# Attention with four query buffers instead of two, and queries asked for three groups in advance

## The chip, the cores and the metric

The kernel runs on one core of a Trainium2 chip. The metric is the time on the device of one execution, in microseconds (us). Engines are named as in the profile: PE (matrix products), DVE (vector), ACT (activations), POOL (GpSimd), SP (the queue that issues most of the transfers). PEld is the loading of PE's weights.

## What is computed

One layer of a decoder in float32, for 2048 tokens of width 1024: attention with latent projections beside a short convolution, an output projection, a layer of 32 experts of which each token takes two, a gated embedding, and norms. The change lies in the attention alone. For each of 8 heads and each block of queries:

```python
s = (einsum('bqhd,bkhd->bhqk', q_nope[:, q0:q1], k_nope[:, :q1])
     + einsum('bqhr,bkr->bhqk', q_rope[:, q0:q1], k_rope[:, :q1]))
...
s = jnp.where(mask, s * scale, -jnp.inf)
pr = jax.nn.softmax(s, axis=-1)
outs.append(einsum('bhqk,bkhd->bqhd', pr, v[:, :q1]))
```

The mask is causal, so that a query sees the keys up to its own place.

## The kernel before

The layer runs in stages: `project` makes queries, keys and values and stores them in DRAM, each split into two float32r parts, high and low; `attention` reads them back; then come the output projection, the routing, the experts and the last norm. Stages follow one another on the engines, but the transfers and the tail of one run beside the head of the next, and a buffer of one stage lies where a buffer of the stage before it lay, and must wait for that one's last use.

**Groups and steps.** Attention goes head by head (h = 0 to 7), and in a head by groups g = 0 to 3 of 512 queries, written (h,g) here. Group (h,g) needs the key chunks 0 to g of 512 keys each, so that it has 4(g + 1) steps: 4, 8, 12, 16 for the four groups, 40 a head. In each step PE makes the scores of 128 queries against 512 keys (L629 to L631: three products, high by high, high by low, low by high), transposes a block of probabilities of 15 steps ago (L655), and multiplies a block of 22 steps ago with the values (L666). DVE takes maxima (L634) and the low part of the transposed blocks (L66), ACT the exponentials (L643) and the high part (L65). The order of every engine but SP's landings is fixed by the text of the program; it is written out by hand (`manual_schedule`).

**Loads.** SP issues in order, and an issue waits until the buffer that it fills is free; what stands behind it waits too. `load_q(h, g)` (L596, L597) fetches 384 KB of queries into one of 2 buffers (`qp`, L569). `load_k(h, c)` (L585, L586) fetches 384 KB of keys into one of 6. `load_v(h)` (L590) fetches 1 MB into one of 2. They are asked for in `scores`, at a group's first step (L601 to L612): at g = 0 the key chunks 2 and 3 of this head; at g = 3 the chunks 0 and 1 and the values of the next head; and last, at each group, the queries of the next one. So the queries of (h,1) are asked for when (h,0), the shortest group, begins, behind two key chunks, and into the buffer that (h-1,3) has just left.

**The end of a group.** When the 16 exponentials of a group are summed, DVE makes the reciprocals (`sm`, L674, L675; 2 buffers). POOL then, in its own order: stores `sm` into DRAM, transposed, in elements of 4 bytes (`rd<-sm`, L681); reads it back along the other axis for 64 partitions (`rb<-rd`, L683), for which it waits until the store has landed; takes the values' sum from `lo`, where ACT has copied it out of its bank (L694; 2 buffers): copy (L695), addition (L696), multiplication with `rb` (L697), store of the result (`od<-o`, L698). PE has one bank for the values' sum, so that the next group's first product (L666) waits for ACT's copy, and ACT's copy waits until POOL has done with `lo` of two groups before. On POOL the order of a head is: `rd` and `rb` of (h-1,3); `rd` and `rb` of (h,0); the products of (h-1,3) and of (h,0); `rd`, `rb`, products of (h,1); the same of (h,2). For h = 1 to 4 POOL also issues a clearing store of 2 MB (L711).

Of the kernel before, what the change touches and what calls it, by code (L numbers as in the profile page):

```python
# [31 lines left out]
# rows of the experts' outputs: the first 128 of each expert, then the next 64 of each;  # L32
# those past 192 go in blocks of 128 of their own
# [3 lines left out]
# units of weights on chip, as loaded and split  # L37
# [4 lines left out]
# tiles of p @ w_ple_proj that wait until the experts are done  # L42
# [3 lines left out]
def row_bc(ap, n):  # L46
    """A DRAM row of n elements, read by every partition."""
    return bass.AP(tensor=ap.tensor, offset=ap.offset, ap=[[0, 128], [1, n]])


class Kernel:
# [7 lines left out]
    def split(self, hi, lo, src, lo_eng=None, hi_eng=None, later=None):  # L59
        """hi + lo = src, each of them exact in float32r; lo only noted where it is for later."""  # L60
        nc = self.nc
        if hi_eng:
            hi_eng.tensor_copy(hi, src)
        else:
            nc.scalar.activation(hi, src, AF.Copy)  # L65
        f = lambda: (lo_eng or nc.vector).tensor_tensor(lo, src, hi.bitcast(F32), op=OP.subtract)  # L66
        f() if later is None else later.append(f)

    def mm3(self, ps, terms, start=True, stop=True):
        """ps += sum of (ah + al)^T (bh + bl), al^T bl aside."""  # L70
        mm, n = self.nc.tensor.matmul, len(terms)
        for i, (ah, al, bh, bl) in enumerate(terms):
            mm(ps, ah, bh, start=(start and i == 0), stop=False)  # L73
            mm(ps, ah, bl, start=False, stop=False)  # L74
            mm(ps, al, bh, start=False, stop=(stop and i == n - 1))  # L75

    def acc(self, ps, prods):
        """ps = the sum of products."""
        for i, (l, r) in enumerate(prods):
            self.nc.tensor.matmul(ps, l, r, start=i == 0, stop=i == len(prods) - 1)  # L80

    def rsqrt_steps(self, pool, r, v):
        """r = v ** -0.5, from an integer guess and three Newton steps; stops between two of them."""
        V = self.nc.vector
        t = pool.tile([128, r.shape[1]], F32, name="rsq_t", bufs=2)
        ri = r.bitcast(I32)
        V.tensor_scalar(ri, v.bitcast(I32), 1, None, op0=OP.logical_shift_right)
        yield
        V.tensor_scalar(ri, ri, -1.0, float(0x5F3759DF), op0=OP.mult, op1=OP.add)
        for _ in range(3):  # L90
            yield
            V.scalar_tensor_tensor(t, r, -0.5, r, op0=OP.mult, op1=OP.mult)
            yield
            V.tensor_tensor(t, t, v, op=OP.mult)
            yield
            V.scalar_tensor_tensor(r, t, 1.5, r, op0=OP.add, op1=OP.mult)
# [6 lines left out]
    def rms_steps(self, pool, r, ss, n):  # L103
        """r = 1 / sqrt(ss / n + EPS), by columns."""
        v = pool.tile([128, ss.shape[1]], F32, name="rms_v", bufs=2)
        self.nc.vector.tensor_scalar(v, ss, 1.0 / n, EPS, op0=OP.mult, op1=OP.add)
        yield
        yield from self.rsqrt_steps(pool, r, v)
# [62 lines left out]
    def project(self, st):  # L171
# [52 lines left out]
        # gains and taps as columns: q 0-2, kv 3-4, taps 5-16 (tap, channel tile)  # L224
# [5 lines left out]
        # rows of the rotary tables: frequency, phase in turns, phase; 64 of cosines, 64 of sines  # L230
# [8 lines left out]
        # sums of every 32nd row  # L239
# [26 lines left out]
        def up_weights():  # L266
            # tiles of 128 columns: 0-3 two heads each without rotation, 4-5 the rotated halves of four heads each
# [176 lines left out]
        def start():  # L444
            """The first tokens' way to the first columns, in the order in which they come."""
# [90 lines left out]
    def rope_angles(self, f512, pi, rcol):  # L536
        """Angles within a turn, for positions pi, a row's kind given by rcol."""
# [17 lines left out]
        # a turn more or less where the first guess was a little off  # L555
# [10 lines left out]
    def attention(self, st):  # L566
        tc, nc = self.tc, self.nc
        kp = self.pool(st, "a_k", 6)
        qp = self.pool(st, "a_q", 2)  # L569
# [29 lines left out]
        def scores(h, g, qi, c):  # L599
            """Scores of 128 queries and 512 keys; with the last of a row's, its softmax."""  # L600
            if c == 0 and qi == 0:  # L601
                if (h, g) == (0, 1):
                    load_v(0)
                if g == 0:
                    load_k(h, 2)
                    load_k(h, 3)
                if g == 3 and h + 1 < H:
                    load_k(h + 1, 0)
                    load_k(h + 1, 1)
                    load_v(h + 1)  # L610
                if (h, g) != hg[-1]:
                    load_q(*hg[hg.index((h, g)) + 1])  # L612
                G = groups[h, g] = dict(pt={}, q=qs_.pop((h, g)))
                G["P"] = [(p3 if g == 3 else p012).tile([128, (g + 1) * 512], F32, name=f"P{g}") for _ in range(4)]
                if g == 1 and R1 + h * 512 - 512 in range(R1, R2):
                    clear(R1 + h * 512 - 512)
                G["rs"] = wk.tile([128, 4, NG], F32, name="rs", bufs=3)
# [53 lines left out]
        def sums(h, g):  # L671
            """1 / the softmax's sums."""
            sm = groups[h, g]["sm"] = wk.tile([128, 4], F32, name="sm")
            nc.vector.tensor_reduce(sm, groups[h, g]["rs"][:, :, :g + 1], axis=AX.X, op=OP.add)  # L674
            nc.vector.reciprocal(sm, sm)  # L675

        def sums_row(h, g):
            """The same along the free axis, on a head's partitions."""
# [6 lines left out]
        def normalise(h, g):  # L685
            """o^T of a head and 512 queries."""
# [28 lines left out]
        load_k(0, 0)  # L715
        load_k(0, 1)
        for n in range(len(s_seq) + lag_v):
# [5 lines left out]
            # a group's last product goes first: what comes next waits for its bank  # L723
# [12 lines left out]
    def ring(self, st):  # L736
        """Weights in units of [128, 1024]: NRAW as they come, NSPLIT split, both used in turn."""
# [13 lines left out]
    def split_unit(self, scale=None, pool=False, later=None):  # L751
        """The next unit's parts, its rows multiplied by scale."""
# [16 lines left out]
    def mix_out(self, st):  # L769
# [50 lines left out]
        # constants of the norm and of the routing; router weights, both levels side by side, hi and lo  # L820
# [31 lines left out]
        # kept: weights, expert and rank of a token's two choices  # L852
# [15 lines left out]
        def trans(t):  # L868
            """xn^T, split, two tiles of tokens side by side."""
# [12 lines left out]
        def logits(t):  # L882
            """Router logits of tiles t and t + 1, transposed; the parts of hi and lo weights below each other."""
# [14 lines left out]
        def route(t0, n):  # L898
            """The choices of n tiles of tokens, and their rows; a step at a time."""
# [13 lines left out]
            def first(hot, d, w, k):  # L913
                """The first of the zeros in d, one-hot."""
# [25 lines left out]
            # one-hot experts, ranks among an expert's tokens  # L940
# [27 lines left out]
            # places in the lists; a far token's is past their end  # L968
# [28 lines left out]
        def go(k=-1, ranks=False):  # L997
            """k steps of the routing, or all (-1); past the ranks' products only if told so."""
# [81 lines left out]
        # the last tiles' way to the lists, beside tiles of p @ w_ple_proj  # L1080
# [38 lines left out]
        # counts of tokens, and of blocks of 128 past FAR  # L1119
# [11 lines left out]
        # rows and weights of a token's two choices, nought if it is far  # L1131
# [22 lines left out]
    def ple_prep(self, wk, t, pst, keep=None):  # L1154
        """p^T of a tile, split; or only kept."""
# [27 lines left out]
    def unit_loads(self, most=NRAW):  # L1183
        """Loads of weights as far ahead as there is room."""
# [34 lines left out]
    def gather(self, e, r):  # L1219
        """The rows of an expert's first 128 tokens (r = 0) or the next 64; where there is none, a row is left."""  # L1220
# [17 lines left out]
    def experts(self, st):  # L1238
# [8 lines left out]
        def half(ps, n, out=None):  # L1247
            """The sum of the two halves' rows."""
# [6 lines left out]
        def block(e, more):  # L1255
            """An expert's first 128 rows; with more, 64 others, their hi and lo side by side."""
# [10 lines left out]
            def free(pool=False):  # L1267
                """A unit is done with: the next in line takes its place."""
                self.next_unit(pool)

            def prods(j, r):
                """Unit j's products, for the first rows (r = 0) or the others."""
# [19 lines left out]
            def hidden(f, r):  # L1292
                """The hidden layer's columns of half f, and where they go transposed."""
# [67 lines left out]
            # the places of the expert before's last two units, and of all but the last two of this one's  # L1361
# [28 lines left out]
    def far_experts(self, st):  # L1390
# [3 lines left out]
        # apart from where the experts start  # L1394
# [6 lines left out]
        with tc.If(nov > 0):  # L1401
            cum = wk.tile([128, E], F32, name="cum")
            V.tensor_tensor_scan(cum, self.ones[:, :E], nb, 0.0, op0=OP.mult, op1=OP.add)
            # the expert of a block
# [10 lines left out]
            # rows of the far tokens  # L1415
# [82 lines left out]
    def finish(self, st):  # L1498
# [124 lines left out]
        # sums of squares: of tile t - 2 (after the embedding) and t + 2 (before)  # L1623
# [37 lines left out]
        # the last tile in parts  # L1661
# [86 lines left out]
```

## Time and profile before

| what | us |
|---|---|
| time of three runs: 2479.6, 2501.54, 2488.54; median | 2488.54 |
| span of the profiled execution | 2492.2 |
| PE busy in it | 2313.6 (93%) |
| DVE busy | 1728.2 (69%) |
| ACT busy | 1341.4 (54%) |
| POOL busy | 701.6 (28%) |

The profiled execution is one of its own; its time outside the span is not given, and its span lies 3.7 us above the median of the three runs. Busy time doesn't count waits: an engine that issues a transfer and then waits for another one to land is idle in this table. Attention takes the stretch from 550 to 1085 us. In rows with a bracket, its number is the engine's idle time just before the instruction and the name what ended it.

### The profile page before, as it was taken

The numbers are of one execution on the slowest core, as the hardware profiler recorded it, in microseconds if no ns is written. First come the engines' busy times: TensorE is split into PE (matmuls) and PEld (weight loads), VectorE is DVE, ScalarE is ACT, GpSimd is POOL, SyncE is SP. The second block draws the span as 40 slices with busy tenths as digits, with TensorE's granted clock in tenths as the row PEclk, the third lists the DMA queues.
The fourth block names the chain that finished last, engine by engine and source line by source line (L and its number), as shares of the span: only waits on it lengthen the run. The fifth ranks groups of instructions, "written<-read, shape, count | busy, mean of one in ns | idle before, by whom it ended". The sixth has DMA issues, their size and how long they took to land. (4 is left out here: it accounts for less than half of the span.)

```text
span 2492.2 us, 34982 instructions
## 1 busy us (share of the span) xinstructions
PE 2313.6 (93%) x12058; PEld 1904.2 (76%) x12058; DVE 1728.2 (69%) x3007; ACT 1341.4 (54%) x2409; POOL 701.6 (28%) x671
## 2 busy tenths in 40 slices
PE   7999999989999999979997998999999999999997
PEld 5878787877787777768785777877787878787775
DVE  6746556537777777767676777667666776776887
ACT  5333333326777777742224666656656665665434
POOL 2121212122233333352333233213322232223342
PEclk9999999998999999999998998999999999999999
DMA  7363635355545444465656789778877887784562
GB/s 216 104 207 102 200 98 180 89 164 105 113 109 118 117 80 80 104 136 183 204 176 209 265 284 317 250 236 285 273 225 245 294 277 262 254 298 148 169 203 94
DMA packets 298378, 465.68 MB, mean 187 GB/s; under 512 B 28105, under 2 KB 198130, under 8 KB 298130
## 3 DMA queue, kind: packets, MB, share of 16 engines
q1 hardware_dynamic: 254304, 333.56, 44.6%
q0 software_dynamic: 36304, 105.39, 13.0%
q10 hardware_dynamic: 7522, 23.61, 2.5%
q8 instruction: 133, 2.18, 0.4%
q14 instruction: 115, 0.94, 0.1%
HBM read 369.04 MB, written 97.62 MB: 187 GB/s over the span
## 5 line engine op out<-in xcount | busy, mean ns | idle before, releaser
L66 DVE TENSOR_TENSOR ul<-raw,uh 128x1024 fp32r<-128x1024 f32 x326 | 465.7, 1446 | 189.3 <-ACT uh L65 175.5
L65 ACT ACTIVATE uh<-raw 128x1024 fp32r<-128x1024 f32 x396 | 403.3, 1052 | 85.7 <-PE bank L1286 36.8
L73 PE MATMUL bank<-uh,xh 128*128 128x256 f32 (+1 forms) x768 | 253.4, 330 | 21.1 <-ACT uh L65 12.1
L74 PE MATMUL bank<-ul,xh 128*128 128x256 f32 (+1 forms) x768 | 249.4, 325 | 3.6 <-issue 3.6
L75 PE MATMUL bank<-uh,xl 128*128 128x256 f32 (+1 forms) x768 | 248.8, 324 | 2.6 <-issue 2.6
L66 POOL TENSOR_TENSOR ul<-raw,uh 128x1024 fp32r<-128x1024 f32 x70 | 170.2, 2433 | 278.2 <-ACT uh L65 242.8
L66 DVE TENSOR_TENSOR pt<-tr,pt 128x512 fp32r<-128x512 f32 (+2 forms) x320 | 194.6, 610 | 76.5 <-ACT pt L65 73.3
L65 ACT ACTIVATE pt<-tr 128x512 fp32r<-128x512 f32 (+2 forms) x317 | 168.9, 533 | 116.5 <-PE tr L655 111.9
L634 DVE TENSOR_REDUCE mx<-s 128x1 f32<-128x512 f32 (+2 forms) x320 | 192.7, 603 | 45.5 <-PE s L631 40.1
L73 PE MATMUL mm<-xh,wh 128*128 128x512 f32 x536 | 212.2, 398 | 6.9 <-ACT xh L65 6.9
L75 PE MATMUL mm<-xh,wl 128*128 128x512 f32 x536 | 212.0, 396 | 0.0
L74 PE MATMUL mm<-xl,wh 128*128 128x512 f32 x536 | 211.8, 395 | 0.0
L666 PE MATMUL av<-pt,v 128*128 128x512 f32 (+3 forms) x640 | 207.1, 408 | 1.4 <-ACT lo L694 1.4
L643 ACT ACTIVATE P<-s,mx 128x512 f32<-128x512 f32 (+2 forms) x320 | 198.8, 622 | 11.5 <-DVE mx L639 11.5
L65 ACT ACTIVATE wh<-raw 128x1024 fp32r<-128x1024 f32 x68 | 72.0, 1060 | 219.0 <-PE mm L74 184.7
L655 PE MATMUL tr<-ident,P 128*128 128x128 f32 x1088 | 180.6, 283 | 0.0
L73 PEld LDWEIGHTS bank<-uh,xh 128*128 128x128 f32 x768 | 147.0, 191 | 38.9 <-issue 24.3
L629 PE MATMUL s<-k,q 96*128 96x512 f32 (+2 forms) x320 | 131.9, 412 | 36.2 <-DMA q<-qrd 27.3
L75 PEld LDWEIGHTS bank<-uh,xl 128*128 128x128 f32 x768 | 147.2, 192 | 18.4 <-issue 6.2
L74 PEld LDWEIGHTS bank<-ul,xh 128*128 128x128 f32 x768 | 147.4, 192 | 14.0 <-issue 1.1
L66 DVE TENSOR_TENSOR xl<-tr,xh 128x512 fp32r<-128x512 f32 x160 | 106.0, 684 | 70.8 <-ACT xh L65 69.6
L655 PEld LDWEIGHTS tr<-ident,P 128*128 128x128 f32 x1088 | 134.7, 146 | 24.9 <-issue 2.0
(371 smaller groups left out, 5587.5 us busy)
## 6 DMA issues: line engine op xcount, KB each, us to landing
raw<-in_w_gate_dram SPq DMA_DIRECT2D x128, 512.0 KB
raw<-in_w_up_dram SPq DMA_DIRECT2D x128, 512.0 KB
raw<-in_w_down_dram SPq DMA_DIRECT2D x128, 512.0 KB
raw<-in_w_in_dram SPq DMA_DIRECT2D x68, 512.0 KB
yd<-y POOLq DMA_DIRECT2D x32, 512.0 KB
xr<-in_x_dram SPq DMA_DIRECT2D x16, 512.0 KB
kd<-stg POOLq DMA_DIRECT2D x16, 512.0 KB
vd<-stg POOLq DMA_DIRECT2D x16, 512.0 KB
```

Of the source, the lines that this page charges most:

```text
L65: nc.scalar.activation(hi, src, AF.Copy)
L66: f = lambda: (lo_eng or nc.vector).tensor_tensor(lo, src, hi.bitcast(F32), op=OP.subtract)
L73: mm(ps, ah, bh, start=(start and i == 0), stop=False)
L74: mm(ps, ah, bl, start=False, stop=False)
L75: mm(ps, al, bh, start=False, stop=(stop and i == n - 1))
L629: mm(s, qh, k[:, 0, :w], start=True, stop=False)
L634: nc.vector.tensor_reduce(mx[:, c:c + 1], s, axis=AX.X, op=OP.max, negate=(g == 0))
L643: nc.scalar.activation(G["P"][qi][:, j * 512:j * 512 + s.shape[1]], s, AF.Exp, bias=nm, accum_out=G["rs"][:, qi, j:j + 1])
L655: nc.tensor.transpose(ps[:, jj], G["P"][qi][:, j * 128:j * 128 + 128], self.ident)
L666: mm(G["av"][:, q0:], heads[h]["v"][:, j], G["pt"][jq][:, hl, jj, q0:], start=(j == 0 and hl == 0), stop=(j == 4 * g + 3 and hl == 1))
```

## The change

`qp` has 4 buffers instead of 2. At a group's first step the queries of the group three further on are asked for, before the keys and the values; the line that asked for the next group's queries last is gone. Before the first step the queries of (0,1) and (0,2) are asked for, between and behind the first key chunks. Nothing is computed otherwise. (The rest of the diff takes out comments.)

```diff
-        qp = self.pool(st, "a_q", 2)
+        qp = self.pool(st, "a_q", 4)
...
             if c == 0 and qi == 0:
+                ahead = hg.index((h, g)) + 3
+                if ahead < len(hg):
+                    load_q(*hg[ahead])
                 if (h, g) == (0, 1):
                     load_v(0)
...
-                if (h, g) != hg[-1]:
-                    load_q(*hg[hg.index((h, g)) + 1])
...
         load_q(0, 0)
         load_k(0, 0)
+        load_q(0, 1)
         load_k(0, 1)
+        load_q(0, 2)
```

SP's order where head 1 begins, before: the rows from the values of head 1 (asked for at group (0,3)) to the queries of (1,2). The numbers tell the buffers' uses apart.

```order
L590 DMA v_4575<-vd_83 128x16x128
L596 DMA q_4577<-qd0_72 64x1024
L597 DMA q_4577<-qrd0_76 32x1024
L585 DMA k_4859<-kd0_78 64x1024
L586 DMA k_4859<-krd_82 32x1024
L585 DMA k_4862<-kd0_78 64x1024
L586 DMA k_4862<-krd_82 32x1024
L596 DMA q_4865<-qd0_72 64x1024
L597 DMA q_4865<-qrd0_76 32x1024
```

Here q_4577 holds the queries of (1,0), the two k the chunks 2 and 3 of head 1, and q_4865 the queries of (1,1), last in the line that (1,0) starts. The same place now:

```order
L596 DMA q_4575<-qd0_72 64x1024
L597 DMA q_4575<-qrd0_76 32x1024
L585 DMA k_4578<-kd0_78 64x1024
L586 DMA k_4578<-krd_82 32x1024
L585 DMA k_4581<-kd0_78 64x1024
L586 DMA k_4581<-krd_82 32x1024
L590 DMA v_4584<-vd_83 128x16x128
L596 DMA q_4865<-qd0_72 64x1024
L597 DMA q_4865<-qrd0_76 32x1024
L585 DMA k_4868<-kd0_78 64x1024
L586 DMA k_4868<-krd_82 32x1024
```

Now q_4575, asked for at (0,3), holds the queries of (1,2), and the keys and values of head 1 stand behind it; q_4865, asked for at (1,0), holds those of (1,3), and chunks 2 and 3 of head 1 stand behind it. The queries of (1,1) went out at (0,2), those of (2,0) go out at (1,1).

The second place is ACT's, where attention begins: the last two splits of the projection, then the exponentials' table and the first exponential. Before:

```order
L65 ACTIVATE stg<-mm 128x512 [waits DMASW4_49,DMASW5_49,DVE_49,PE_49]
L65 ACTIVATE stg<-mm 128x512 [waits DMASW6_49,DMASW7_49,DVE_49,PE_49]
L643 ACT_TABLE_LOAD
L643 ACTIVATE P_4304,rs<-s,mx 128x128 [waits DVE_49]
L643 ACTIVATE P_4305,rs<-s,mx 128x256 [waits DVE_49]
```

and now:

```order
L65 ACTIVATE stg<-mm 128x512 [waits DMASW4_49,DMASW5_49,DVE_49,PE_49]
L65 ACTIVATE stg<-mm 128x512 [waits DMASW6_49,DMASW7_49,DVE_49,PE_49]
L644 ACT_TABLE_LOAD [waits DMASW2_49,DVE_49]
L644 ACTIVATE P_4310,rs<-s,mx 128x128 [waits Activation_49]
L644 ACTIVATE P_4311,rs<-s,mx 128x256 [waits DVE_49]
```

No instruction moved on ACT, but the two more buffers push the buffers behind them along, so that those of the maxima and of the exponentials' sums now lie where the projection's last results (`stg`) lay. The table's loading, which waited for nothing, now waits for a store of POOL's (DMASW2) and for DVE's first maximum, which has the same new wait. The orders of PE, DVE and POOL are unchanged.

## Rows read from the trace of the kernel before

**Rows 1.** Waits from 550 to 1085 us: engine line, waited for: total, times, longest.

```profile
POOL rb L683 <- DMA rd<-sm: 284.7, 31, 13.5
...
PE s L629 <- DMA q<-qrd: 27.3, 7, 5.3
...
ACT lo L694 <- POOL o L696: 3.7, 3, 1.8
...
PE av L666 <- ACT lo L694: 1.4, 2, 1.0
```

**Rows 2.** PE in order of time: first, second and last of the seven waits for queries.

```profile
621.78 0.77 PE L629 MATMUL s<-k,q 96*128 96x512 f32 x1 [5.29 <-DMA q<-qrd]
...
685.31 0.47 PE L629 MATMUL s<-k,q 96*128 96x512 f32 x1 [3.25 <-DMA q<-qrd]
...
1009.45 0.47 PE L629 MATMUL s<-k,q 96*128 96x512 f32 x1 [3.67 <-DMA q<-qrd]
```

**Rows 3.** Stretches from PE's restart past the clock's rise: first, longest, last of seven.

```profile
core 0: us, PE busy (x) PEld busy (x) DVE busy (x) ACT busy (x) POOL busy (x), PEclk, DMA share, GB/s
621.78:629.00 7.22, 7.22 (x30) 6.34 (x31) 3.08 (x6) 3.26 (x8) 3.00 (x4) 0.56 0.88 297
...
751.70:763.00 11.30, 11.30 (x47) 9.91 (x48) 5.45 (x11) 5.45 (x14) 2.60 (x3) 0.58 0.09 17
...
1009.45:1015.00 5.55, 5.55 (x28) 5.11 (x29) 2.56 (x6) 2.94 (x8) 2.62 (x3) 0.69 0.18 37
```

**Rows 4.** POOL's waits alone, from 638.5 to 1028.5 us.

```profile
POOL rb L683 <- DMA rd<-sm: 225.2, 24, 13.5
POOL o L697 <- DMA rb<-rd: 27.0, 11, 4.2
POOL rd L681 <- DVE sm L675: 8.4, 2, 8.1
POOL od L698 <- POOL o L697: 7.1, 24, 0.3
POOL yd L711 <- issue: 0.9, 1, 0.9
POOL rd L681 <- issue: 0.2, 1, 0.2
```

**Rows 5.** POOL in order of time, single instructions.

```profile
626.53 0.60 POOL L695 COPY o<-lo 64x512 f32<-64x512 f32 x1 [4.05 <-ACT lo L694]
...
638.79 0.81 POOL L681 DMA_DIRECT2D rd<-sm  x1 [8.06 <-DVE sm L675]
...
716.88 0.53 POOL L683 DMA_DIRECT2D rb<-rd  x1 [13.49 <-DMA rd<-sm]
...
770.20 0.81 POOL L681 DMA_DIRECT2D rd<-sm  x1 [0.37 <-DVE sm L675]
...
1021.36 0.53 POOL L683 DMA_DIRECT2D rb<-rd  x1 [7.38 <-DMA rd<-sm]
...
1028.10 0.79 POOL L681 DMA_DIRECT2D rd<-sm  x1
```

**Rows 6.** DVE's reciprocals of the sums, from 638 to 1029 us.

```profile
L675 DVE RECIPROCAL sm<-sm x25: 178/178/179, 638.3 to 1024.6; 128x4 f32<-128x4 f32 x25
```

**Rows 7.** SP in order of time: the first values; keys and queries where (1,0) begins.

```profile
547.79 0.38 SPq L590 DMA_DIRECT2D v<-vd  x1
...
605.26 0.45 SPq L585 DMA_DIRECT2D k<-kd  x1
...
610.39 0.57 SPq L597 DMA_DIRECT2D q<-qrd  x1
```

**Rows 8.** ACT: two waits, at attention's start and in head 2.

```profile
558.36 0.60 ACT L65 ACTIVATE stg<-mm 128x512 fp32r<-128x512 f32 x1 [7.16 <-DMA qrd<-stg]
...
561.55 1.28 ACT L643 ACT_TABLE_LOAD   x1
...
730.87 0.60 ACT L694 ACTIVATE lo<-av 128x512 f32<-128x512 f32 x1 [1.76 <-POOL o L696]
```

**Rows 9.** PE's wait at attention's start, in order of time.

```profile
559.74 0.80 PE L629 MATMUL s<-k,q 96*128 96x512 f32 x1 [6.54 <-DVE stg L66]
```

**Rows 10.** The stretch around that wait.

```profile
547.00:559.00 12.00, 5.61 (x29) 4.36 (x27) 3.38 (x6) 2.81 (x5) 5.39 (x7) 0.89 0.78 214
```

## The prediction

> **What bounds the kernel now.** I read the attention stretch alone, since nothing else changes. First its waits, longest in total first. [rows 1] show the wait that the change is aimed at: PE stood 27.3 us, seven times, for queries. In order of time [rows 2] these are single waits, 5.29 the longest and 3.9 on the mean (27.3 / 7), one a head from head 1 on, where (h,1) starts: the queries asked for at 610.39 [rows 7] let PE go on at 621.78, 11.4 us later. Behind each, the granted clock fell to its lower level (1.2 GHz) and rose again some microseconds after PE had restarted. [rows 3] measure it: stretch times (1 - clock) gives 7.22 x 0.44 = 3.2 us lost in the first, 11.30 x 0.42 = 4.7 in the longest, 5.55 x 0.31 = 1.7 in the last, and 19.1 over the seven. So PE alone would gain 27.3 + 19.1 = 46.4 us.
>
> But the longest row of [rows 1] is POOL's: 284.7 us in 31 waits of POOL for its own `rd` to land. POOL is busy for 28% of the span, and looks idle. So I asked for POOL's waits alone over six heads, from the `rd` of (0,3) at 638.79 to that of (6,3) at 1028.10 [rows 4, 5]. In these 389.3 us POOL waited 225.2 us for `rd` to land, 27.0 for `rb`, 7.1 for its own work, 1.1 for issuing, and for another engine's work only 8.4 us: 8.06 of it ends at the first row of the stretch, and 0.37 at 770.20. Everything else is POOL's chain, link after link: store `sm`, wait about 9.4 us (225.2 / 24), fetch `rb`, three operations, store, and the next group's `rd` without a pause. It takes 389.3 / 6 = 64.9 us a head, and it doesn't get shorter when PE is faster.
>
> PE's own need over the same six heads is less. The reciprocals, which follow PE, go from 638.3 to 1024.6 [rows 6], 386.3 us. Six of the seven waits for queries lie in there, 27.3 - 5.3 = 22.0 us, and 19.1 - 3.2 = 15.9 of the half-clock loss. Without them PE, DVE and ACT would take 348.4, or 58.1 us a head, 6.8 less than POOL.
>
> Do the two meet? Yes: ACT's copy into `lo` waits for POOL's addition of two groups before, and PE's next product waits for that copy. [rows 1] have ACT waiting for POOL three times, up to 1.8 us, and PE for ACT twice; one of these is at 730.87 in head 2 [rows 8]. POOL's chain already touches PE, lightly because the waits for queries hold PE to nearly the same pace.
>
> **The change part by part.** *The seven waits.* The queries of (h,1) now go out at (h-1,2), 28 steps before (h,0) begins, into a buffer that is free by then. Their wait goes, and with it the fall of the clock there. What is late next is POOL. PE can run ahead by what the two buffers of `lo` and of `sm` give: `lo` of (h,1) needs POOL's addition of (h-1,3). From the `rd` of (1,3) on, where POOL already lagged, PE's gain of 6.8 us a head turns into a wait of about that size on POOL, or into one of DVE on `sm`, whose two buffers are free only when the `rd` of two groups before has landed. Only what lies before the saturated stretch is kept. There POOL itself waited for PE: 4.05 us at 626.53 and 8.06 at 638.79 [rows 5]. The first gap, with its clock, made both late: 5.3 + 3.2 = 8.5 us. Without it the products at 626.53 start 4.05 sooner, `sm` of (0,3) is ready 8.5 sooner, and POOL, then still with some 3.6 us to spare, stores it 8.5 sooner. With the 0.37 at 770.20 that is 8.9 us off the chain. In POOL's order the last products stand ahead of its part of the next stage's weights, so I let the end move by the same.
>
> *Keys and values behind the queries.* The queries of (h,3) wait for the end of (h-1,3), and the key chunks 2 and 3 stand behind them. They left at 605.26 [rows 7], 5 us before (h,0) began; now they leave at its start. Chunk 2 is needed 14 steps later, some 20 us (64.9 us / 40 steps is 1.6 each). The transfer of queries at that place took 11.4 us, so it is hidden with about 9 us to spare; if it weren't, the 6.8 us a head that PE has spare would hide that much. The next head's keys and values now leave at the start of (h,3), 16 steps or some 25 us before their first use. I cost both at nothing.
>
> *The landings of `rd`.* They share the engines with these loads, and the trace doesn't show them at the new places. From below: all 24 at the shortest row, 7.38 us, would take 24 x 2.0 = 48 us off the chain, and PE would be the bound again. From above: two of a head's four at the longest, 13.49 instead of 9.4, over six heads, cost 12 x 4.1 = 49 us. I take no change: a head still loads four times queries, four key chunks and one block of values, some near an `rd` and some not, and the mean of 24 holds both kinds.
>
> *The start.* PE waits 6.54 us at 559.74 for a split [rows 9] that waits 7.16 us for the projection's store to land [rows 8], in a stretch where the transfers run at 0.78 of all engines and 214 GB/s [rows 10]. The 1 MB of values asked for there at 547.79 [rows 7] now stands behind the queries of (1,0), which wait for (0,0): 1.05 MB / 214 GB/s = 4.9 us of transfers leave the way. Against it, the first maximum and the table now wait for a store to land, and the table's 1.28 us [rows 8], hidden before, stands behind the maximum. Bounds: 6.5 us gained, or one store's landing of about 7 us and the table, 8 lost. I take 2 us gained: 4.9 - 1.3 = 3.6, and of that some half, since the new wait for a store takes an unknown part.
>
> *Sum.* 8.9 + 2 = 10.9 us off the profiled execution's 2492.2, or 2481.3. That execution's span lies 3.7 us above the median of the three runs; from the median 2488.5 it is 2477.6, say **2478 us**, 0.4% less. A measurement of this kernel can tell about 1%, 25 us, from no change.
>
> A rule speaks against this. The rows have `rd`, 512 elements of 4 bytes, landing in 9.4 us on the mean, 7.38 where shortest [rows 4, 5]. The Trainium skill, DMA: Bandwidth & Descriptors, section Anatomy of one DMA, gives a transfer from GpSimd's queue 2.0 us and its bytes at 436 GB/s, which makes 2.0 us for these 2 KB, an estimate from that page; the chain would then be 7.4 x 4 = 30 us a head shorter and would not bind, and all of PE's 46.4 us would show. The trace disagrees with it for these 4-byte elements, so the sum goes by the row.
>
> **The rivals.** *A: POOL doesn't bind.* Then 46.4 + 2 = 48.4 us, 2440. It needs POOL's loop to fall by 6.8 us a head, 1.7 a landing, nearly the whole way to the shortest row. For it: `rd` of (6,2) landed in 7.38. Against it: the same loads remain.
>
> *B: some loads leave the landings' way.* Two of a head's four at 7.38: 6 x 2 x 2.0 = 24 us more, 2454. For it: loads of (h,1) no longer share the place with those of the keys. Against it: queries, two key chunks and values, 2.2 MB, are now asked for in one go.
>
> *C: slower.* That one go falls, at the pace of POOL's chain, on the `rd` of (h-1,3) and of (h,0). The row at 716.88 shows 13.49 us with loads and the clearing store about [rows 5]. The saving is gone when a head's chain grows by 10.9 / 6 = 1.8 us; two landings a head at 13.49 give 49 - 10.9 = 38 us more than now, 2527; one gives 14 more, 2502. Against it: the landings with loads near them are in the mean already. The Trainium skill, DMA: Bandwidth & Descriptors, section Queues, rings and completion order, says that each transfer engine takes the queues in turn, a packet at a time; by that rule a burst on SP's queue stretches POOL's store, which gives C its chance.
>
> *D: the wait only moves,* to chunk 2 of the keys. It would be hidden in PE's spare 6.8 us a head, and the time is the forecast's.
>
> **How the numbers follow.** Forecast with D 0.74, A 0.08, B 0.12, C 0.06. Faster by over 1%: A and B, 0.20; within 1%: 0.74; slower: 0.06. For the range, the forecast with its start (6.5 gained to 8 lost) and a landing's drift of half a microsecond (12 us) reaches from 2461 to 2500; B lies below, so I go to 2450 and leave A and C out.
>
> **What would show it.** Right: no PE waits for queries; in their place PE waits behind ACT's `lo`, or DVE behind `sm`, about 5 us a head from head 2 on, with the clock falling there; POOL's chain from the `rd` of (1,3) still about 65 us a head without outside waits; landings still about 9.4. Wrong: attention shorter by 40 us, POOL waiting for `sm` in every head; landings under 8 or over 11 on the mean.

## The result, and the profile after

| | before | after |
|---|---|---|
| median of the runs, us | 2488.54 (2479.60 to 2501.54) | 2509.25 (2505.48 to 2517.04) |
| ratio | | 1.0075, 95% interval 1.0051 to 1.0098 |
| span of the profiled execution | 2492.2 | 2507.7 |
| mean granted clock | 0.966 | 0.966 |

The change makes the kernel 0.75% slower, where 0.4% faster was forecast; 2509 lies above the range's end of 2500. First the waits of attention after the change, from 550 to 1105 us, since attention now ends later (engine line, waited for: total, times, longest; rows left out are marked).

```profile
POOL rb L684 <- DMA rd<-sm: 291.9, 31, 12.9
...
POOL o L698 <- DMA rb<-rd: 54.5, 13, 6.8
DVE sm L675 <- DMA rd<-sm: 32.8, 9, 7.4
PEld tr L656 <- DVE pt L66: 24.1, 8, 6.3
ACT lo L695 <- POOL o L697: 22.9, 7, 4.8
PE tr L656 <- DVE pt L66: 22.7, 6, 6.2
...
PE av L667 <- ACT lo L695: 17.1, 7, 4.0
```

(Lines from L613 on stand one higher than before.) The 27.3 us of PE's waits for queries in [rows 1] are gone. In their place DVE waits 32.8 us for the `rd` of two groups before, because `sm` has two buffers, and PE waits 22.7 us behind DVE; ACT waits 22.9 us for POOL's addition, where it waited 3.7, and PE 17.1 behind ACT, where it waited 1.4. So PE now waits for POOL.

POOL's waits alone, over the same six heads as [rows 4], from the `rd` of (0,3), now at 636.75, to that of (6,3), now at 1042.00:

```profile
POOL rb L684 <- DMA rd<-sm: 227.3, 24, 12.9
POOL o L698 <- DMA rb<-rd: 41.2, 9, 6.7
POOL od L699 <- POOL o L698: 7.4, 25, 0.3
POOL yd L712 <- issue: 0.9, 1, 0.9
```

These heads take 405.3 us, 67.5 a head instead of 64.9, and no wait in them is for another engine: POOL sets the pace. The 24 landings of `rd` are what they were (227.3 against 225.2). That sum hides an exchange: over six heads the `rd` of (h,0) waits 8.0 us more and that of (h,2) 3.4, the `rd` of (h-1,3) 7.6 less and that of (h,1) 1.7. What grew in total is the other wait of the chain, for `rb`: 41.2 against 27.0. The span's 15.5 us are found by the time of three rows: the `rd` of (0,3) comes 2.0 sooner, the six heads take 15.9 more (14.2 of them for `rb`, 2.1 for `rd`), and 1.6 are left behind (6,3).

All of the growth lies in one place of each head, the multiplication of (h,1); the other waits for `rb` together fell by 3.1. Its waits over heads 1 to 6 were 3.99, 2.81, 2.26, 2.25, 4.24, 2.91 and are 6.02, 6.74, 5.64, 5.36, 6.37, 5.71: 35.8 instead of 18.5. POOL's rows for (1,1), and its multiplication there before:

```profile
667.78 0.79 POOL L682 DMA_DIRECT2D rd<-sm  x1
677.32 0.53 POOL L684 DMA_DIRECT2D rb<-rd  x1 [8.75 <-DMA rd<-sm]
...
685.90 1.28 POOL L698 TENSOR_TENSOR o<-o,rb 64x512 f32<-64x512 f32 x1 [6.02 <-DMA rb<-rd]
```

```profile
685.88 1.26 POOL L697 TENSOR_TENSOR o<-o,rb 64x512 f32<-64x512 f32 x1 [3.99 <-DMA rb<-rd]
```

POOL is here most of a head behind PE, so that the line of SP that stands ahead of this fetch is the one that the next head starts. First and last of its eight issues after the change: the queries of (2,3), two key chunks of head 2, the queries of (3,0), 1.5 MB in 7.8 us, the last issue 1.0 us ahead of the fetch of `rb`. Before, the line was two key chunks of head 2 and the queries of (2,1), 1.15 MB, the last issue at 675.97, 3.4 us ahead of that fetch at 679.35.

```profile
670.00 0.45 SPq L596 DMA_DIRECT2D q<-qd  x1
...
676.28 1.55 SPq L597 DMA_DIRECT2D q<-qrd  x1
```

The distance is not what the heads have in common: in heads 2 to 6 before, the last issue stands only 0.1 to 1.9 us ahead, and the waits are the shorter ones. The amount goes with it. In the 10 us ahead of the fetch SP asked for 0.77 to 1.15 MB before and for 1.15 to 1.54 MB now. It doesn't set the wait alone: with 1.15 MB ahead, POOL waited 2.9 and 4.0 us before and 5.4 to 6.4 now.

At the start, the table's loading and the first `rd` (ACT, then POOL), against 561.55 without a wait in [rows 8]:

```profile
562.98 1.28 ACT L644 ACT_TABLE_LOAD   x1 [5.28 <-DVE mx L635]
...
581.36 0.78 POOL L682 DMA_DIRECT2D rd<-sm  x1 [18.36 <-DVE sm L676]
592.39 0.56 POOL L684 DMA_DIRECT2D rb<-rd  x1 [10.26 <-DMA rd<-sm]
...
601.73 1.28 POOL L698 TENSOR_TENSOR o<-o,rb 64x512 f32<-64x512 f32 x1 [6.77 <-DMA rb<-rd]
603.87 0.78 POOL L682 DMA_DIRECT2D rd<-sm  x1
```

The first `rd` is 1.4 us late (579.92 before). It lands in 10.26 instead of 6.62, `rb` in turn makes POOL wait 6.77 instead of nothing, and the second `rd` is 8.9 us late (595.00 before).

### The profile page after: what moved, and what is told of

It is laid out like the page before. It is cut to its first block, busy times and chain, and to the rows that moved or that the text cites. A ratio compares the mean times of both kernels' runs of the same rounds, so it can differ in the third digit from the quotient of the medians.

```text
span 2507.7 us, 34954 instructions
## 1 busy us (share of the span) xinstructions
PE 2313.5 (92%) x12058; PEld 1900.7 (76%) x12058; DVE 1726.9 (69%) x3007; ACT 1340.1 (53%) x2409; POOL 699.0 (28%) x671
## 5 line engine op out<-in xcount | busy, mean ns | idle before, releaser
L667 PE MATMUL av<-pt,v 128*128 128x512 f32 (+3 forms) x640 | 211.1, 414 | 17.1 <-ACT lo L695 17.1
L644 ACT ACTIVATE P<-s,mx 128x512 f32<-128x512 f32 (+2 forms) x320 | 199.0, 622 | 11.2 <-DVE mx L640 11.1
L656 PE MATMUL tr<-ident,P 128*128 128x128 f32 x1088 | 178.0, 280 | 22.7 <-DVE pt L66 22.7
L630 PE MATMUL s<-k,q 96*128 96x512 f32 (+2 forms) x320 | 129.8, 406 | 12.7 <-ACT P L644 10.5
```

Source lines behind the costliest of these rows:

```text
L630: mm(s, qh, k[:, 0, :w], start=True, stop=False)
L644: nc.scalar.activation(G["P"][qi][:, j * 512:j * 512 + s.shape[1]], s, AF.Exp, bias=nm, accum_out=G["rs"][:, qi, j:j + 1])
L656: nc.tensor.transpose(ps[:, jj], G["P"][qi][:, j * 128:j * 128 + 128], self.ident)
L667: mm(G["av"][:, q0:], heads[h]["v"][:, j], G["pt"][jq][:, hl, jj, q0:], start=(j == 0 and hl == 0), stop=(j == 4 * g + 3 and hl == 1))
```

## Experiments

Theories: **1** POOL's chain binds, and the requests that now go out together make it longer. **2** The loss comes from attention's start, where the buffers were pushed along. **3** Queries fetched earlier crowd the landings wherever they stand in the line. **4**, formed after the first group: the 4-byte store of `rd` also crowds the loads, and PE's waits for queries came from that. The kernel before didn't take the same time in all groups of runs (2533.7, 2513.2, 2514.9, 2493.2 and 2517.3 us), so times are compared by their ratio to the kernel before on the same chip; brackets are 95% intervals. Chain means POOL's time a head, from the `rd` of (0,3) to that of (6,3).

**What of the change costs.** Four buffers alone, with the old requests:

```diff
-        qp = self.pool(st, "a_q", 2)
+        qp = self.pool(st, "a_q", 4)
```

> The kernel before with four query buffers and its old order of requests. Theory 1 (POOL's chain binds; the change lengthens it because queries, two key chunks and values go out in one burst): SP is no longer held by the query buffer, so the queries of (h,1) leave with the key chunks about 5 us before (h,0), and PE's waits for queries shrink below 1 us each; POOL's chain stays near 65 us a head (rd of (0,3) to rd of (6,3): 385 to 393 us); the time is 2480 to 2495. Theory 2 (the loss comes from the shift of the buffers at attention's start, whose new waits stand here too): 2500 to 2510, with the first rd as late as after the change and 8 us lost by the rd of (0,1). Theory 3 (any queries fetched earlier crowd the landings): the chain is at 67 us a head, 2500 or more.

Measured: 1.0044 [1.0025, 1.0063]. PE still waited 16.9 us for queries, seven times, so the buffer was not all that held them: theory 1 had expected less than 1 us each. The chain was 70.9 us a head on this chip. For the `rb` of (h,1) POOL waited 29.9 us over heads 1 to 6, and the loss is about what the moved buffers alone cost (1.0036, further below).

The changed kernel with the queries asked for last:

```diff
             if c == 0 and qi == 0:
-                ahead = hg.index((h, g)) + 3
-                if ahead < len(hg):
-                    load_q(*hg[ahead])
...
                     load_v(h + 1)
+                ahead = hg.index((h, g)) + 3
+                if ahead < len(hg):
+                    load_q(*hg[ahead])
```

> The changed kernel, the queries still three groups in advance but asked for behind the keys and values of a group's first step, so that keys and values no longer wait for the query buffer. Theory 1: the one burst of 2.2 MB at (h,3) and the one of 1.2 MB at (h,0) come apart, the waits for rb of (h,1) fall from about 6 us back to about 3, the chain from 67.5 to about 65 us a head, and the time to 2490 to 2500 (the start's loss stays). Theory 2 (start): chain and start unchanged, 2505 to 2512. Theory 3 (earlier queries crowd the landings wherever they stand in the line): chain 67 us a head, 2505 to 2512.

> The changed kernel with the queries asked for last, once more, to read its profile beside that of the kernel before on the same chip. Theory 1: ratio 0.998 to 1.003 again; POOL's chain within 1 us a head of the kernel before, waits for rb within 5 us of it over the six heads, what is left of a loss at the start.

Measured: 1.0001 [0.9982, 1.0021], and again 1.0020 [0.9998, 1.0042]. PE never waits for queries, but nothing is lost, and nothing gained. Theory 3 falls. The landing that had grown is short again, as theory 1 expected: in the two profiles the waits for `rb` of (h,1) are 15.4 and 16.0 us over heads 1 to 6, with 0.38 to 0.90 MB asked for in the 10 us ahead of the fetch. Of the second, the multiplication of (1,1):

```profile
681.17 1.28 POOL L698 TENSOR_TENSOR o<-o,rb 64x512 f32<-64x512 f32 x1 [2.23 <-DMA rb<-rd]
```

But another grew: queries and two key chunks now go out ahead of the fetch of `rb` of (h,2) (in heads 1 to 5 of the two profiles 1.15 MB in the 10 us ahead of it, once 0.77, and at most 0.38 in the two kernels of the first pair), and POOL waits 21.2 and 19.4 us for it over heads 1 to 6, where it waited 6.5 before the change and 5.4 after it. Here too more requests ahead of the fetch go with a later landing.

The changed kernel itself, and the kernel before, on the next chip:

> The changed kernel, once more, on the chip of this group. Theory 1: ratio to before 1.005 to 1.010 again, POOL's chain 2 to 3 us a head longer than that of the kernel before on the same chip, more than half of it in the waits for rb. Rival (the loss is one chip's chance): ratio within 0.3% of 1.

> The kernel before, once more, for its profile beside the runs of this group. On the chip of the first four runs it took 2533.7 instead of 2488.5. Theory 1 (POOL's chain sets attention's pace): on a slower chip the landings of rd are longer and the chain is about 68 to 69 us a head. Rival: the chain is 65 and the difference lies outside attention.

Measured: 1.0105 [1.0076, 1.0134]: the loss is not one chip's. POOL's waits over the six heads, of the kernel before and then of the changed one:

```profile
POOL rb L683 <- DMA rd<-sm: 247.5, 24, 13.8
POOL o L697 <- DMA rb<-rd: 31.7, 12, 4.9
```

```profile
POOL rb L684 <- DMA rd<-sm: 243.7, 24, 13.0
POOL o L698 <- DMA rb<-rd: 42.7, 10, 6.6
```

`rd` lands no later than before (243.7 against 247.5), and `rb` again costs some 11 us more, with 36.6 instead of 20.6 at (h,1). The chain is 69.3 and 70.5 us a head, 7.2 us over the six heads where the first pair had 15.9, and the `rd` of (0,3) is 6.0 late. On this slower chip the kernel before has no wait of POOL for `sm` at (0,3) (8.06 us in [rows 5]), so that there was no gap to take up the start.

Now the start by itself. First the new buffers behind all others, so that nothing is pushed along:

```diff
-        qp = self.pool(st, "a_q", 4)
+        qp = [self.pool(st, "a_q", 2)]
...
         wk = self.pool(st, "a_wk", 2)
+        qp.append(self.pool(st, "a_q2", 2))
...
-            q = qs_[h, g] = qp.tile(
+            q = qs_[h, g] = qp[g % 2].tile(
```

> The changed kernel with the two new query buffers behind all other buffers, so that none is pushed along: the table's loading and the first maximum wait for no store of the projection any more. Theory 2 for the start alone (the pushed buffers make the first rd some 3 us late, and POOL's chain carries that to the end): ratio to before 1.004 to 1.008, 3 to 8 us below the change's 1.0075 to 1.0105, with the first rd near 580 and the chain unchanged at 67 to 71 us a head. Rival (the start is late because the three first queries and the values crowd it): rd of (0,1) as late as in the changed kernel, ratio 1.007 or more.

Measured: 1.0122 [1.0099, 1.0145], and inconclusive: at the start PE now waited 11.1 us for queries, and SP, ahead of their load, 39.8 us for a store of the projection. A wait went and a longer one came. (For the `rb` of (h,1) POOL again waited 35.5 us over heads 1 to 6.) The kernel before with 8 KB left empty behind its query buffers does it the other way round:

```diff
         qp = self.pool(st, "a_q", 2)
+        self.pool(st, "a_pad", 1).tile([128, 2048], F32, name="pad")
```

> The kernel before with 8 KB a partition left unused behind its two query buffers, so that all buffers behind are pushed along as by the change, and the table's loading and the first maximum wait for a store of the projection; requests are as before. If the shift makes the start late: first rd 3 us later than in the kernel before, ratio 1.001 to 1.003, and the chain unchanged. If the start's loss comes from the requests instead: ratio 0.998 to 1.001, first rd within 1 us.

> The kernel before, for its profile beside these runs: the chain at 68 to 70 us a head as on the chip of the other groups, seven or six waits of PE for queries of some 25 us.

Measured: 1.0036 [1.0013, 1.0059]. Of this kernel ACT's table, and POOL's first `rd`:

```profile
568.13 1.28 ACT L644 ACT_TABLE_LOAD   x1 [4.89 <-DVE mx L635]
...
586.51 0.78 POOL L682 DMA_DIRECT2D rd<-sm  x1 [18.36 <-DVE sm L676]
```

The first `rd` is 7.2 us later than in the kernel before on this chip (579.36), but by the `rd` of (0,3) only 1.9 us of that are left (637.30 against 635.39). The other 7.7 us by which the span of this profile is longer come later, 6.5 of them in the six heads. So a shift that touches no request costs 0.1 to 0.6%, and theory 2 holds for a part; that the start is where it costs this isn't shown. The rest should be in the requests: keys asked for one group later,

```diff
-                if g == 0:
+                if g == 1:
                     load_k(h, 2)
                     load_k(h, 3)
```

> The changed kernel with the key chunks 2 and 3 asked for at the first step of (h,1) instead of (h,0), so that the line at (h,0) holds queries alone. Theory 1 with the burst at (h,0) as its cause: the waits for rb of (h,1) fall from about 6 us to about 3, the chain becomes 1 to 2 us a head shorter than the changed kernel's, ratio 1.000 to 1.005. Rival (the burst only moves to the next rd and rb): waits for rb fall at (h,1) and rise at (h,2), ratio 1.006 to 1.012. If the keys come late: PE waits for chunk 2 at (h,2), over 2 us a head.

Measured: 1.0010 [0.9989, 1.0031], the time that theory 1 expected. But its profile doesn't show the reason: the waits for `rb` of (h,1) are still 2.5 to 6.2 us, the chain is 67.3 us a head against 64.1 in the kernel before on that chip, and its stretch behind (6,3) is 8 us shorter. With the queries last the chain was 65.6, with `rb` at 35.4 us against 26.9. One profile each can't settle differences of this size. The changed kernel didn't run on this chip; by the ratios (up to 1.0031 and 1.0042, where the changed kernel has at least 1.0051) both other orders of asking take most or all of the loss back. With the queries last, the landing of `rb` at (h,1) falls with it; that this alone wins the time back isn't shown.

**Whether PE's gain was there.** The store of `rd` as 128 runs of 16 bytes, in the changed kernel and in the one before:

```diff
-            q.dma_start(self.rd[h, g].rearrange("(a b) -> b a", b=128), G["sm"])
+            q.dma_start(self.rd[h, g].rearrange("(b a) -> b a", a=4), G["sm"])
...
-            nc.gpsimd.tensor_tensor(o[A], o[A], G["rb"][A], op=OP.mult)
+            ov, rv = o[A].rearrange("p (a b) -> p a b", a=4), G["rb"][A].rearrange("p (b a) -> p a b", a=4)
+            nc.gpsimd.tensor_tensor(ov, ov, rv, op=OP.mult)
```

> The changed kernel with the store of the sums' reciprocals as 128 runs of 16 bytes instead of 512 elements of 4, and the multiplication reading rb in that order. Theory 1: the landing falls from 9.4 to some 3 to 6 us, POOL's chain would need 45 to 55 us a head and no longer binds; PE's own pace of about 58 us a head shows, with no waits for queries and none for lo: 2440 to 2460. Rival (the landing is a fixed cost, not one of its 512 elements): landing 8 us or more, time within 10 us of the change's 2509. Rival (PE is held by something else than POOL): landing shorter, chain still over 64 us a head with POOL waiting for sm, 2490 or more.

> The kernel before with the same 16-byte store. Theory 1: POOL no longer binds, but the seven waits of PE for queries and the half clock behind them stay (46 us in all), so that the time falls little, 2475 to 2490, about 64 us a head, with POOL waiting for sm; the difference to the changed kernel with that store is then 20 to 45 us in favour of the change. Rival (queries were never worth 46 us): both kernels with that store come out within 10 us of each other.

Measured: 0.9640 [0.9614, 0.9666] with the change, 0.9614 [0.9590, 0.9638] without, 2441.7 and 2436.2 us on one chip. Both run at 57.6 us a head. POOL's waits over the six heads of the kernel before with this store:

```profile
POOL o L695 <- ACT lo L694: 85.2, 24, 7.7
POOL rb L683 <- DMA rd<-sm: 76.0, 24, 5.4
POOL rd L681 <- DVE sm L675: 44.8, 13, 6.7
```

`rd` lands in 3.2 us on the mean (76.0 / 24) and POOL waits for ACT and DVE: it no longer binds. From 640 to 1000 us the kernel before, and then the same with this store (columns as in [rows 3]):

```profile
640.00:1000.00 360.00, 339.00 (x1978) 280.80 (x1978) 271.65 (x565) 265.63 (x700) 114.35 (x135) 0.95 0.49 101
```

```profile
640.00:1000.00 360.00, 360.00 (x2216) 299.65 (x2215) 302.33 (x629) 295.49 (x781) 135.32 (x157) 1.00 0.43 114
```

PE is busy without a pause at the full 2.4 GHz, with two query buffers and the old requests: not one wait for queries is left to remove. The expectation for the kernel before (that its seven waits would stay) was wrong, and with it the reason for the change.

Why did they go? Landings, of the changed kernel with the old store and with the new (KB each, median us from issue to landing):

```profile
q<-qd SPq DMA_DIRECT2D x32, 256.0 KB, 5.2
k<-kd SPq DMA_DIRECT2D x32, 256.0 KB, 9.2
...
q<-qrd SPq DMA_DIRECT2D x32, 128.0 KB, 10.2
k<-krd SPq DMA_DIRECT2D x32, 128.0 KB, 11.0
...
rd<-sm POOLq DMA_DIRECT2D x31, 2.0 KB, 9.4
```

```profile
q<-qd SPq DMA_DIRECT2D x32, 256.0 KB, 4.1
k<-kd SPq DMA_DIRECT2D x32, 256.0 KB, 5.2
...
q<-qrd SPq DMA_DIRECT2D x32, 128.0 KB, 3.8
k<-krd SPq DMA_DIRECT2D x32, 128.0 KB, 5.3
...
rd<-sm POOLq DMA_DIRECT2D x31, 2.0 KB, 1.9
```

SP's loads are not touched by the edit and land sooner, three of the four rows in about half the time or less. To part crowding from POOL's waiting, the kernel with the 16-byte store got each back alone. The 4-byte store, which nobody waits for, on ACT's queue (`re` is a second array in DRAM):

```diff
             q.dma_start(self.rd[h, g].rearrange("(b a) -> b a", a=4), G["sm"])
+            nc.scalar.dma_start(self.re[h, g].rearrange("(a b) -> b a", b=128), G["sm"])
```

> The kernel before with the 16-byte store, and beside it the old store of 512 elements of 4 bytes once a group, on ACT's queue, into a place that nobody reads. POOL waits only for the 16-byte store. Theory 1 alone (POOL's chain is all that the 4-byte store costs): within 8 us of the 2436 without it, no waits for queries. Theory 4 (the 4-byte elements crowd the transfer engines, so that every load near them lands late, and the seven waits for queries came from that): waits of PE for queries come back, the landings of keys and queries and of the 16-byte store grow by several us, and the time is 2445 to 2490.

Measured: 0.9941 [0.9915, 0.9966], 2499.6 us. PE's waits for queries are back, and `rd`, though in runs of 16 bytes, lands in 7.8 us on the mean (186.6 / 24). From the waits of attention:

```profile
POOL rb L685 <- DMA rd<-sm: 248.3, 30, 16.6
...
PE s L630 <- DMA q<-qrd: 24.8, 7, 5.2
```

As control the same second store in runs of 16 bytes, and the kernel without it:

```diff
-            nc.scalar.dma_start(self.re[h, g].rearrange("(a b) -> b a", b=128), G["sm"])
+            nc.scalar.dma_start(self.re[h, g].rearrange("(b a) -> b a", a=4), G["sm"])
```

> The kernel before with the 16-byte store, and beside it a second store of the same 2 KB on ACT's queue that nobody reads, as 128 runs of 16 bytes instead of 512 elements of 4. If the number of elements crowds the transfer engines: no waits of PE for queries, ratio to before 0.960 to 0.970, within 10 us of the kernel without the second store. If a further store on ACT's queue does it, whatever its shape: waits for queries of some 25 us, ratio 0.990 or more.

> The kernel before with the 16-byte store, once more, beside the run with the second store: ratio to before 0.958 to 0.970, attention at 57 to 58 us a head, no waits of PE for queries.

Measured: 0.9708 [0.9651, 0.9765] and 0.9694 [0.9637, 0.9752], 57.9 and 57.6 us a head; one wait for queries of 1.6 us with the second store. So it is the 512 elements that crowd the loads, and not one more store on that queue.

And POOL's waiting without the crowding:

```diff
+            if q is nc.gpsimd:
+                for _ in range(14):
+                    nc.gpsimd.tensor_tensor(junk, nought, nought, op=OP.add)
             rb = G["rb"] = wk.tile([128, 512], F32, name="rb")
```

> The kernel before with the 16-byte store, and on POOL 14 additions without use (some 9 us) between the store of rd and the fetch of rb, so that POOL's chain is as long as with the 4-byte store and the transfer engines are left alone. Theory 1: the chain binds again at 60 to 66 us a head, with DVE waiting for sm's buffers or ACT for lo's, PE without waits for queries, and the time is 2455 to 2490. Theory 4 alone (crowding is what costs, not POOL's chain): within 8 us of the 2436 without the additions.

Measured: 0.9863 [0.9839, 0.9886], 2479.6 us. The additions hold POOL for 9.6 us a group. From the waits of attention:

```profile
ACT lo L697 <- POOL o L699: 23.1, 6, 5.3
...
PE av L666 <- ACT lo L697: 18.2, 6, 4.5
```

The chain is 63.4 us a head, POOL waits for other engines 1.8 us in six heads, and PE waits behind ACT behind POOL, with no wait for queries. POOL's chain by itself binds.

Last, the change where the 4-byte elements crowd but POOL doesn't wait for them (the changed kernel with the 16-byte store and the stray 4-byte one):

> The changed kernel with the 16-byte store and, beside it, the store of 512 elements of 4 bytes on ACT's queue that nobody waits for: to be read beside the same addition to the kernel before, ratio 0.994, where PE waited 24.8 us for queries and POOL's chain had 32 us of waits for PE. If landings stayed as they are, the change would save those gaps: 20 to 35 us, ratio 0.981 to 0.986, PE without waits for queries. If the change's burst of requests lengthens the landings as it does in the plain kernels: waits for queries gone, POOL's waits for rd and rb longer by 2 us a head or more, ratio 0.988 to 1.000.

Measured: 0.9939 [0.9916, 0.9963], the 0.9941 of the kernel without the change. From its waits of attention:

```profile
POOL rb L686 <- DMA rd<-sm: 260.7, 31, 15.4
...
POOL o L701 <- DMA rb<-rd: 68.2, 17, 9.7
ACT lo L697 <- POOL o L699: 27.6, 6, 7.7
```

PE's 24.8 us for queries are gone, POOL's waits for `rb` rise from 47.6 to 68.2, and PE waits behind `lo`: the same exchange as in the plain kernels, here with a net of nothing.

One more tried for a better version (16-byte store, queries asked for last, buffers as in the run with a_q2):

> The changed kernel with the 16-byte store, queries asked for behind keys and values, and no buffer pushed along. Theory 1 with theory 4: without the 4-byte elements PE waits for nothing that the change could bring earlier, so the time is that of the kernel before with the 16-byte store, ratio 0.958 to 0.965. Rival (with landings short, early queries do gain): ratio below 0.955.

Measured: 0.9702 [0.9683, 0.9722], with the 10.8 us wait for the first queries that the place of those buffers brings, and 57.6 us a head. The version that beats both kernels is the kernel before with the 16-byte store alone: 2436.2 and 2437.5 us, 3.9 and 3.1% less than before.

## Why the prediction was wrong, point by point

- **PE's waits for queries go; POOL binds:** right. PE has none, POOL none for another engine from (0,3) on, and the new waits stand where they were named: behind `lo` and behind `sm`. With POOL held 9.6 us a group and nothing crowded, the chain alone set the pace.
- **PE's own need, 58.1 us a head:** right; with the 16-byte store both kernels take 57.6.
- **The landings, "I take no change":** the step that failed. The sum over `rd` did hold (227.3 against 225.2). But the chain has a second landing, `rb`, whose 27.0 us stood in the rows and got no bound of its own. It became 41.2: 14.2 us, more than the whole forecast gain. The argument that a head's loads are the same counted bytes and not where they stand: with two blocks of queries where one stood, the line that (h+1,0) starts brings up to 1.54 MB instead of at most 1.15 into the 10 us ahead of the fetch of `rb` of (h,1). That the order of asking lengthens that landing is borne out by its waits, over heads 1 to 6: 35.5 to 36.6 us in three profiles with this order, 17.6 to 20.6 in three of the kernel before, and 15.4 and 16.0 with the queries asked for last; that it is the whole of the loss is not.
- **Rival C, slower by the one burst:** right in sign and kind, and 0.06 was far too little. It looked at the `rd` of (h-1,3) and (h,0): the second did grow, by 8.0 us over six heads, but the first fell by 7.6. The landing that made the chain longer was the `rb` of (h,1), behind the line that (h+1,0) starts. Its decision point, 1.8 us a head, was passed: 15.9 / 6 = 2.65.
- **The first gap, 8.9 us kept:** with the start's 2 us, the `rd` of (0,3) was to come 10.5 sooner (the other 0.37 lie at 770.20); it came 2.0 sooner (636.75 instead of 638.79). PE's wait before it is gone, but attention's start came later.
- **The start, 2 us gained:** wrong in sign. The first `rd` is 1.4 late, the second 8.9. The new wait of the table was named, and its bound, 8 lost, covers the first and nearly the second. The shift alone costs 0.1 to 0.6%, though its own profile has only 1.9 us of it at the `rd` of (0,3); the rest of the start was not tried apart.
- **Where the waits for queries come from:** never asked. I read 11.4 us from issue to use as the price of a load, when it was the price of a load beside 512 elements of 4 bytes. With that store gone the waits go, without the change; with it put back unwaited they return.
- **The 2.0 us for such a store,** which the prediction gave as an estimate from the Trainium skill (DMA: Bandwidth & Descriptors, section Anatomy of one DMA), were set aside by the row, rightly for 4-byte elements. In runs of 16 bytes the same 2 KB landed in 1.9 us in the median of the changed kernel and in 3.5 in the kernel before. The Trainium skill, DMA: Bandwidth & Descriptors, section Rules for kernel authors, says that a strided last dimension makes one descriptor per element and should be rearranged to be contiguous. The runs agree, with 9.4 us before such a rearrangement and 1.9 after it, both in the changed kernel.
- **The sum:** forecast 10.9 us off 2492.2; measured 15.5 on. The difference of 26.4 is 8.5 at the `rd` of (0,3), which came 2.0 instead of 10.5 sooner, 16.3 in the six heads (15.9 more instead of 0.4 less), and 1.6 behind (6,3).

Open: how much of the loss each landing carries, since with the queries last `rb` of (h,2) grows where `rb` of (h,1) falls and yet the time comes back; why a shift of buffers costs time behind the start; and how the start's late second `rd` divides between the shift and the three early queries.

## What to carry to other kernels

When an engine waits for a load, ask first what makes the load slow, and only then whether it can be asked for earlier: here the load shared the transfer engines with a small store in 4-byte elements, and mending that store was worth 3 to 4% where asking earlier cost 0.75 to 1.05. A chain of small transfers on an engine that is busy 28% of the time can be the bound; each landing in it needs a term and bounds of its own, and what is issued just ahead of each must be looked up in the new order, not averaged over the old one. Two more buffers also move all that lie behind them, and a moved buffer can bring a wait at a stage's border.

## What the runs showed of the hardware that was not expected

Packets of 4 bytes slow other queues far beyond their own share. SP's queue from 640 to 1000 us in the kernel before with the 16-byte store, and then, with the stray 4-byte store beside it, SP's queue and ACT's (packets, MB, share of 16 engines):

```profile
q1 hardware_dynamic: 19136, 27.53, 29.1%
```

```profile
q1 hardware_dynamic: 18307, 24.50, 37.8%
...
q10 hardware_dynamic: 12672, 0.05, 2.1%
```

And SP's queue with the second store in runs of 16 bytes:

```profile
q1 hardware_dynamic: 18861, 26.56, 30.6%
```

The stray packets (12672 of them, 0.05 MB) took 2.1% themselves, but a MB of SP's took 1.54% of the engines' time instead of 1.06% (37.8 / 24.50 and 29.1 / 27.53). With the same 2 KB in runs of 16 bytes it took 1.15% (30.6 / 26.56), and without a second store on that same chip again 1.06% (29.2 / 27.53), so that most of the rise comes with the 4-byte elements. The Trainium skill, DMA: Bandwidth & Descriptors, section Issuing engines are not separate DMA queues, says that transfers of all issuing engines run on the same 16 engines and interleave. These rows agree, since a store on ACT's queue made a MB of SP's loads cost 1.54% instead of 1.06%.
